# Mixture of experts in a decoder trunk: the pairs of experts in a software pipeline on TensorE

## The chip, the cores and the metric

The kernel runs on one core of a Trainium2 chip. The metric is device time in microseconds (us), the median over runs; lower is better. PE is TensorE, DVE is VectorE, ACT is ScalarE, POOL is GpSimd, and SP is the engine that issues nearly all transfers here.

## What is computed

Two layers of a hybrid decoder over 256 tokens of 1024 features, all in float32. The change lies in the mixture of experts at the end of each layer, which in the reference is:

```
weights = sel / jnp.sum(sel, axis=-1, keepdims=True)          # two experts of 16 for each token
combine = jnp.sum(jax.nn.one_hot(idx, N_EXPERTS) * weights[..., None], axis=1)
def add_expert(acc, p):
    e_w1, e_w3, e_w2, e_c = p                                  # 1024 x 512, 1024 x 512, 512 x 1024
    y = (jax.nn.silu(hf @ e_w1) * (hf @ e_w3)) @ e_w2
    return acc + e_c[:, None] * y, None
```

The rest of a layer (four mixers, gates, the router) is not touched.

## The kernel before

The 16 experts are worked in eight pairs (expert e with e + 8), each pair on 128 slots: four groups of 32 slots, each group on its own quarter of PE's columns. The work of a pair has these steps, and the texts below use these names:

- **gather** (`gather`, once for two pairs): eight blocks of the slots' tokens, feature-major, by a one-hot matrix (L1506 on PE, evacuated in turn by DVE L1510 and ACT L1508); the one-hot transposed (L1521, copied by ACT L1522); the slots' weights (DVE L1514 and L1515, added by POOL L1516, then L1526 on PE).
- **first products** (L1560): eight weight pages, two banks. Then `swiglu`: tanh on ACT (L1473) and two DVE operations (L1474, L1475).
- **transposes** of the hidden activations (`turn`: L1483 on PE into one bank, copied by ACT L1485).
- **second products** (L1584): four weight pages, two banks; DVE scales them (L1591), ACT and DVE split them in high and low halves (L581, L582).
- **token sums** (`combine`): for four pieces of the output, two matmuls (L1537) into one bank each, which DVE adds to x (L1538).

The weights come as 96 pages of 1 MB per layer. `order` lists them, `issue` sends them through SP's queue as soon as a page of SBUF is free, and `done` frees a page after its last matmul. Eight banks of PSUM are shared out by tags: `acc` has three, `mx` two, `rw` three. First products take two of `acc`, second products two of `mx`, the transposes one of `rw`, token sums one of `acc` at a time, a gather `mx` and `rw`. The order of instructions on an engine is not the order of the code: the framework's scheduler places them, and every engine then works its own list strictly in that order, each instruction waiting for its inputs and its bank.

Ahead of the last pair's transposes stands `tc.If(ov > 0)`, a branch of every engine over `dense`, a slow path for counts that the slots can't hold. It isn't entered here, so a branch is taken past it. After the last pair comes the next layer's norm, or the output.

Of the kernel before, what the change touches and what calls it, by code (L numbers as in the profile page):

```python
"""Hybrid decoder trunk: S5, sparse attention, RG-LRU and RWKV-7 mixers, gated merge, grouped MoE."""
# [13 lines left out]
F32R = mybir.dt.float32r                 # 12 significant bits: a float32 is exactly the sum of two  # L15
AF = mybir.ActivationFunctionType
OP = mybir.AluOpType
# [3 lines left out]
P = 128  # L21
L, D, T = 2, 1024, 256
W = 256
KT = D // P
NE, NPAIR, DE = 16, 8, 512
EARLY = [(0, 0), (1, 0)]                 # modulation values by PE instead of DVE: layer, group
NW = 2                                   # buffers of halves of weights
NR, NM = 5, 15                           # pages of 8 KB per partition: of the weight stream, of everything else
KEEP = 1                                 # pages of the latter that the stream leaves free
FILL, SPARE = (2, 2, 2, 2, 1, 3, 3), 2   # work beside the mixers: steps of it per step of them, pages it leaves free  # L30
XAT, MAT_AT = 3, 3                       # pages of the stream that x and the small matrices follow
PLAN = "1311330100b0322d22ac"            # that work: gates of a branch (0 to 3), its merge (a to d)
PSB = dict(acc=3, mx=2, rw=3)            # banks of PSUM: dense products, small ones, RWKV
TM = (164, 256, 256, 256)                # columns of iq | ik | iw, of q, k and v
# [5 lines left out]
# Columns of the per-feature parameters of a layer: name, number of columns.  # L40
# [9 lines left out]
# Small matrices of a layer, side by side.  # L50
# [27 lines left out]
class Pages:  # L78
    """Pages of [128, 2048] float32 in SBUF, whole or in slots of 512; the longest free goes first."""

    def __init__(self, pool, name, n):
        self.tiles = [pool.tile([P, 2048], F32, tag=f"{name}{i}", name=f"{name}{i}") for i in range(n)]
        self.free_pages = list(range(n))
        self.slots = []                 # free slots of split pages: (page, slot)
        self.used = {}                  # page -> slots in use, of split pages
        self.owner = {}
# [60 lines left out]
def _emit(ctx, tc, I, out):  # L147
# [26 lines left out]
    # ------------------------------------------------------------------ weight stream  # L174
# [3 lines left out]
    def fill_plan(l):  # L178
        """What runs beside the mixers: the gates, and modulation values that are needed later."""
# [16 lines left out]
    for l in range(L):  # L196
# [12 lines left out]
        for pr in range(NPAIR):  # L209
            for kt in range(KT):  # L210
                order.append((("w13", l, pr, kt), I["w13"][l, pr, kt], 2048))
            for ft in range(4):
                order.append((("w2", l, pr, ft), I["w2"][l, pr, ft], 2048))
# [37 lines left out]
    # ------------------------------------------------------------------ inputs and constants  # L251
# [45 lines left out]
    # Masks of 64 x 64 tiles: rows (p mod 64) are s, columns t; t > s, t >= s, and the blocks that  # L297
    # the recursive inverse joins.
# [17 lines left out]
    # Slots of a pair (e, e + 8) of experts: 32..95 and then 0..31 for e, 96..127 and then 0..31 for e + 8.  # L316
# [3 lines left out]
    # Of four, an earlier one (last index) also goes before an equal one.  # L320
# [8 lines left out]
    # ------------------------------------------------------------------ small accurate functions  # L329
# [22 lines left out]
    def sincos(sn, cs, ang, shape):  # L352
        """Reduction by quarter turns in parts that multiply exactly, then polynomials."""
# [1188 lines left out]
    def experts(l, x, oh, sid, wts, used, regi, gate2):  # L1542
        now, nxt, last = {}, {}, None
        steps = gather(l, 0, sid, used, nxt)
        for pr in range(NPAIR):
            i = pr % 2
            if i == 0:
                now, nxt = nxt, {}
# [242 lines left out]
```

## Time and profile before

| what | value |
|---|---|
| median of 3 runs | 1261.74 us (1261.24 to 1262.14) |
| span of the profiled execution, from its first to its last instruction | 1258.4 us |
| median of the runs above that span | 3.3 us |
| PE busy | 1105.5 us (88%) |
| DVE busy | 752.8 us (60%) |
| mean rate of transfers | 262 GB/s |

The experts are the stretches from about 399 to 646 us (layer 0) and from about 1002 to 1248 us (layer 1). Times inside the trace are counted from the span's start. An instruction of the program that takes float32 operands shows as two records on PE.

### The profile page before, as it was taken

What the parts mean: (1) busy time and instruction counts of PE and PEld (TensorE: products, weight loads), DVE (VectorE), ACT (ScalarE), POOL (GpSimd) and SP (SyncE); (2) the same over time, 40 slices, a digit from 0 to 9 for tenths busy, and PEclk for the clock granted to TensorE, in tenths of its full rate; (3) what the DMA queues carried; (4) which work ended last, traced back from release to release, by engine and by line L of the source; (5) the groups of instructions that cost most, each with busy time, mean ns of one, the idle gap of its engine ahead of it and who ended that gap; (6) DMA issues with size and microseconds to landing.
All of it is one profiled execution on the core that took longest, in us unless ns stands there. A gap on an engine that the chain in (4) does not pass through costs nothing. (4 is left out here: it accounts for less than half of the span.)

```text
span 1258.4 us, 22758 instructions
## 1 busy us (share of the span) xinstructions
PE 1105.5 (88%) x9286; PEld 722.1 (57%) x9286; DVE 752.8 (60%) x1439; ACT 374.1 (30%) x662; POOL 257.5 (20%) x320
## 2 busy tenths in 40 slices
PE   3878999988986999998849899998898699999894
PEld 0878886856873345332218798886677444443321
DVE  5789995598666134232275899959877623233223
ACT  1543433415432111110026544541354211011101
POOL 0593112151232000000091111115414200000000
PEclk8888999989997999998969899999899799999897
DMA  9635787625564999999803468832346489999951
GB/s 357 232 126 208 294 304 292 244 70 199 179 255 150 362 407 421 421 421 410 323 34 134 137 235 299 302 135 101 140 177 255 165 323 416 421 420 420 419 223 52
DMA packets 47089, 329.83 MB, mean 262 GB/s; under 512 B 5992, under 2 KB 6120, under 8 KB 7552
## 3 DMA queue, kind: packets, MB, share of 16 engines
q1 hardware_dynamic: 45776, 327.47, 66.9%
q8 instruction: 78, 1.28, 0.4%
q10 hardware_dynamic: 1200, 0.79, 0.2%
q14 instruction: 35, 0.29, 0.1%
HBM read 327.19 MB, written 1.05 MB: 261 GB/s over the span
## 5 line engine op out<-in xcount | busy, mean ns | idle before, releaser
L614 PE MATMUL acc<-h_hi,whi 128*128 128x256 f32 x720 | 213.8, 297 | 0.2 <-ACT whi L581 0.2
L614 PE MATMUL acc<-h_hi,wlo 128*128 128x256 f32 x720 | 206.3, 287 | 3.5 <-DVE wlo L582 3.5
L614 PE MATMUL acc<-h_lo,whi 128*128 128x256 f32 x720 | 206.4, 287 | 3.3 <-DVE h_lo L582 3.3
L582 DVE TENSOR_TENSOR wlo<-ring,whi 128x1024 fp32r<-128x1024 f32 (+2 forms) x122 | 152.6, 1254 | 62.7 <-ACT whi L581 54.7
L581 ACT ACTIVATE whi<-ring 128x1024 fp32r<-128x1024 f32 (+2 forms) x122 | 125.9, 1033 | 208.9 <-PE acc L614 145.9
L1560 PE MATMUL acc<-page,page 128*32 128x512 f32 (+1 forms) x1408 | 174.3, 600 | 0.0
L614 PEld LDWEIGHTS acc<-h_hi,whi 128*128 128x128 f32 x720 | 138.6, 192 | 16.8 <-issue 7.4
L614 PEld LDWEIGHTS acc<-h_lo,whi 128*128 128x128 f32 x720 | 139.0, 193 | 7.4 <-DVE h_lo L582 4.1
L614 PEld LDWEIGHTS acc<-h_hi,wlo 128*128 128x128 f32 x720 | 139.0, 193 | 6.7 <-DVE wlo L582 4.5
L1560 PEld LDWEIGHTS acc<-page,page 128*32 128x32 f32 x1408 | 48.8, 110 | 95.2 <-issue 90.8
L1591 DVE SCALAR_TENSOR_TENSOR page<-mx,moslw,page 128x512 f32<-128x512 f32 x32 | 24.0, 751 | 124.9 <-PE mx L1584 124.9
L1584 PE MATMUL mx<-page,page 128*32 (+1 forms) x704 | 87.4, 630 | 5.2 <-ACT page L1485 5.2
L1560 PE MATMUL acc<-ring,page 128*32 128x512 f32 (+1 forms) x640 | 84.7, 595 | 0.0
L468 DVE SCALAR_TENSOR_TENSOR page<-ring,csil,page 128x512 f32<-128x512 f32 x112 | 83.0, 780 | 0.0
L1516 POOL TENSOR_TENSOR page<-page,page 128x512 f32<-128x512 f32 x6 | 7.6, 1271 | 328.4 <-DVE page L1515 233.2
L1538 DVE TENSOR_TENSOR page<-page,acc 128x512 f32<-128x512 f32 x64 | 41.7, 683 | 51.9 <-PE acc L1537 51.2
L1474 DVE SCALAR_TENSOR_TENSOR page<-page,acc 128x512 f32<-128x512 f32 x16 | 11.0, 687 | 96.9 <-ACT page L1473 96.9
L1584 PEld LDWEIGHTS mx<-page,page 128*32 128x32 f32 x704 | 24.1, 116 | 59.3 <-issue 49.1
L581 ACT ACTIVATE wlo<-page 128x512 fp32r<-128x512 f32 x32 | 20.2, 631 | 123.5 <-DVE page L1591 123.5
L1473 ACT ACTIVATE page<-acc 128x512 f32<-128x512 f32 x16 | 9.6, 597 | 154.2 <-PE acc L1560 154.2
L1317 POOL TENSOR_TENSOR page<-page,page 128x512 f32<-128x512 f32 x21 | 32.3, 1557 | 79.3 <-DVE page L1315 78.3
L1537 PE MATMUL acc<-wlo,whi 128*128 128x512 f32 x128 | 44.7, 438 | 2.3 <-ACT wlo L581 1.4
(514 smaller groups left out, 2102.8 us busy)
## 6 DMA issues: line engine op xcount, KB each, us to landing
page<-in_w SPq DMA_DIRECT2D x132, 1024.0 KB, 12.1
ring<-in_w SPq DMA_DIRECT2D x60, 1024.0 KB, 11.3
ring<-in_ada_w SPq DMA_DIRECT2D x48, 1024.0 KB, 5.2
ring<-in_gate_w SPq DMA_DIRECT2D x32, 1024.0 KB, 5.8
ring<-in_branch_w SPq DMA_DIRECT2D x8, 1024.0 KB, 4.8
ring<-in_w_rw SPq DMA_DIRECT2D x6, 1024.0 KB, 10.2
ring<-in_w_tm SPq DMA_DIRECT2D x6, 1024.0 KB, 4.8
ring<-in_w_fm SPq DMA_DIRECT2D x6, 1024.0 KB, 4.8
```

The source lines that it names most:

```text
L468: V.scalar_tensor_tensor(p[:, js], w[:, js], csil[:, kt, 0:1], p[:, js], op0=OP.mult, op1=OP.add)
L581: S.activation(hi, a, AF.Copy)
L582: V.tensor_tensor(lo, a, hi.bitcast(F32), OP.subtract)
L614: PE.matmul(p, w, x_, **f)
L1317: G.tensor_tensor(mix[dp], mix[dp], t, OP.add)
L1473: S.activation(a, h1, AF.Tanh, scale=0.5)
L1474: V.scalar_tensor_tensor(b, a, 1.0, h1, op0=OP.add, op1=OP.mult)
L1537: PE.matmul(p, oh[:, P * a:P * a + P], y[:, fs], start=y is yh, stop=y is yl)
L1538: V.tensor_tensor(x[:, a, fs], x[:, a, fs], p, OP.add)
L1560: PE.matmul(hh[f][32 * g:32 * g + 32, :], xg[:, kt, P * i + 32 * g:P * i + 32 * g + 32], w[:, ds(offs[g] + 512 * f, 512)], start=kt == 0, ...
L1584: PE.matmul(yp[f][32 * g:32 * g + 32, :], gT[:, ft, 32 * g:32 * g + 32], w[:, ds(offs[g] + 512 * f, 512)], start=ft == 0, stop=ft == 3)
L1591: V.scalar_tensor_tensor(t, yp[f], now["w"][:, i:i + 1], gate2[:, fs], op0=OP.mult, op1=OP.mult)
```

## The change

The loop over pairs is cut in two functions, `first(pr)` (gather, first products, swiglu) and `second(pr)` (transposes, second products, halves), and put together so that the code runs first(0); then for each pair first(pr + 1), the token sums of pair pr - 1, second(pr); and the last token sums at the end. Every gather now goes block by block beside the first products of its own even pair; before, this was so for pair 0 alone, and the others were written as a block ahead of the transposes of an odd pair. First products of odd pairs go to `rw` instead of `acc`, transposes of odd pairs to `acc` instead of `rw`. The branch stands after the token sums of pair 6. The pages are listed in the new order of use. Nothing that is computed changes, and no instruction of the path that is taken is added or removed.

```
-        for pr in range(NPAIR):
-            for kt in range(KT):
-                order.append((("w13", l, pr, kt), I["w13"][l, pr, kt], 2048))
-            for ft in range(4):
-                order.append((("w2", l, pr, ft), I["w2"][l, pr, ft], 2048))
+        for pr in range(NPAIR + 1):
+            if pr < NPAIR:
+                order.extend((("w13", l, pr, kt), I["w13"][l, pr, kt], 2048) for kt in range(KT))
+            if pr:
+                order.extend((("w2", l, pr - 1, ft), I["w2"][l, pr - 1, ft], 2048) for ft in range(4))
...
-    def turn(b):
-        p = pt("rw", [P, 4, P])
+    def turn(b, tag="rw"):
+        p = pt(tag, [P, 4, P])
...
     def experts(l, x, oh, sid, wts, used, regi, gate2):
-        now, nxt, last = {}, {}, None
-        steps = gather(l, 0, sid, used, nxt)
-        for pr in range(NPAIR):
-            i = pr % 2
+        packs, regs, hidden, outs = {}, {}, {}, {}
+
+        def first(pr):
+            i, pp = pr % 2, pr // 2
+            steps = None
             if i == 0:
-                now, nxt = nxt, {}
+                o = packs[pp] = {}
+                steps = gather(l, pp, sid, used, o)
...
-            hh = [pt("acc", [P, 512]) for _ in range(2)]
+            hh = [pt("rw" if i else "acc", [P, 512]) for _ in range(2)]
             for kt in range(KT):
-                if pr == 0:
+                if steps:
                     next(steps)
...
-            b = swiglu(hh[0], hh[1])
-            if last:
-                combine(x, *last)
-            if i:
-                M.free(xg)
-                if pr + 1 < NPAIR:
-                    for _ in gather(l, (pr + 1) // 2, sid, used, nxt):
-                        pass
-            if pr == NPAIR - 1:
...
-            gT = turn(b)
+            hidden[pr] = swiglu(hh[0], hh[1])
+
+        def second(pr):
+            i, o, offs = pr % 2, packs[pr // 2], regs.pop(pr)
+            gT = turn(hidden.pop(pr), "acc" if i else "rw")
...
+            outs[pr] = o["oh"][:, i], yh, yl
+
+        first(0)
+        for pr in range(NPAIR):
+            if pr + 1 < NPAIR:
+                first(pr + 1)
+            if pr:
+                combine(x, *outs.pop(pr - 1))
+            if pr == NPAIR - 1:
...
+            second(pr)
```

Three places of PE's list show what the scheduler made of it. In the listing, x4 counts instructions of the program that read alike, one weight page is four rows of products with their ISA rows between, and the changed kernel's lines L1564, L1581 and L1602 are L1560, L1584 and L1576 of the kernel before.

Before, the end of the third gather (pairs 4 and 5) and pair 3's transposes (rw_4651), on PE in layer 0:

```order
L1526 MATMUL rw_4645<-ones_f,page_78 128x1 x4
L1483 MATMUL rw_4651<-identr,page_78 128x128 x2
L1506 MATMUL mx_4627<-whi_4578,h_hi 128x256
L1506 MATMUL mx_4627<-whi_4578,h_lo 128x256
L1506 MATMUL mx_4627<-whi_4578,h_hi 128x256
L1506 MATMUL mx_4627<-whi_4578,h_lo 128x256
L1483 MATMUL rw_4651<-identr,page_78 128x128 x2
L1584 ISA
L1584 MATMUL mx_4657<-page_85,page_78 32x512 x4
```

Now, the end of pair 4's first products and pair 3's transposes (acc_4730), on PE:

```order
L1564 MATMUL acc_4565<-ring_67,page_85 32x512 x4
L1564 ISA
L1564 MATMUL acc_4566<-ring_67,page_85 32x512 x4
L1537 MATMUL acc_4726<-wlo_4554,whi_4198 128x512
L1537 MATMUL acc_4726<-wlo_4555,whi_4198 128x512
L1483 MATMUL acc_4730<-identr,page_77 128x128 x4
L1581 ISA
L1581 MATMUL mx_4736<-ring_68,page_78 32x512 x4
```

The gather has left this place: its blocks stand between pair 4's first products. Pair 3's transposes follow the token sums of pair 2, and its second products follow them with nothing between.

Before, the slots' weights of the fourth gather (rw_5014) and pair 5's transposes (rw_5020), on PE:

```order
L1506 MATMUL mx_4996<-whi_4947,h_hi 128x256
L1506 MATMUL mx_4996<-whi_4947,h_lo 128x256
L1506 MATMUL mx_4996<-whi_4947,h_hi 128x256
L1506 MATMUL mx_4996<-whi_4947,h_lo 128x256
L1526 MATMUL rw_5014<-ones_f,page_78 128x1 x4
L1483 MATMUL rw_5020<-identr,page_78 128x128 x4
L1584 ISA
L1584 MATMUL mx_5026<-ring_67,page_78 32x512 x4
```

Now, the same weights (rw_5074), on PE:

```order
L1521 MATMUL rw_5067<-identr,whi_4936 128x128 x4
L1581 ISA
L1581 MATMUL mx_4885<-ring_70,page_76 32x512 x4
L1581 ISA
L1581 MATMUL mx_4886<-ring_70,page_76 32x512 x4
L1526 MATMUL rw_5074<-ones_f,page_78 128x1 x4
L1581 ISA
L1581 MATMUL mx_4885<-ring_66,page_76 32x512 x4
```

They now stand one weight page deep in pair 4's second products, and pair 5's transposes are elsewhere, ahead of the last page of pair 6's first products.

Before, PE ahead of the branch: the end of pair 7's first products:

```order
L1560 MATMUL acc_5221<-ring_69,page_76 32x512 x4
L1560 ISA
L1560 MATMUL acc_5222<-ring_69,page_76 32x512 x4
L1574 TENSOR_LOAD moregi_3886
L1576 COMPARE_AND_BRANCH
```

Now, PE ahead of the branch:

```order
L1581 MATMUL mx_5250<-page_82,page_76 32x512 x4
L1537 MATMUL acc_5293<-wlo_5285,whi_4936 128x512
L1537 MATMUL acc_5297<-wlo_5285,whi_4936 128x512
L1537 MATMUL acc_5301<-wlo_5285,whi_4936 128x512
L1537 MATMUL acc_5305<-wlo_5286,whi_4936 128x512
L1600 TENSOR_LOAD moregi_3886
L1602 COMPARE_AND_BRANCH
```

Pair 7's first products are done much earlier, and the branch follows the second products and the token sums of pair 6. Pair 7's transposes stand right behind the branch in both.

## Rows read from the trace of the kernel before

**Rows 1.** The page: span, granted clock and transfer rate in 40 slices.

```profile
span 1258.4 us, 22758 instructions
PEclk8888999989997999998969899999899799999897
GB/s 357 232 126 208 294 304 292 244 70 199 179 255 150 362 407 421 421 421 410 323 34 134 137 235 299 302 135 101 140 177 255 165 323 416 421 420 420 419 223 52
```

**Rows 2.** Windows: busy time of each engine (instructions), PE's granted clock, DMA share.

```profile
399.00:500.00 101.00, 100.52 (x827) 43.75 (x827) 30.20 (x58) 13.37 (x23) 2.54 (x2) 0.98 0.94 372
500.00:625.38 125.38, 116.84 (x903) 41.16 (x902) 35.87 (x62) 15.34 (x26) 2.54 (x2) 0.96 0.97 401
1002.00:1102.00 100.00, 99.47 (x821) 43.11 (x820) 30.00 (x65) 14.18 (x25) 2.54 (x2) 0.98 0.92 373
1102.00:1229.77 127.77, 119.22 (x918) 42.64 (x912) 37.86 (x65) 15.71 (x27) 2.55 (x2) 0.96 0.88 362
```

**Rows 3.** Waits of PE, 1002 to 1246 us: total us, times, longest.

```profile
PE rw L1483 <- issue: 3.9, 1, 3.9
PE mx L1584 <- ACT page L1485: 3.8, 5, 0.9
PE rw L1526 <- POOL page L1516: 3.0, 1, 3.0
PE rw L1483 <- DVE page L1475: 1.4, 1, 1.4
...
PE acc L1537 <- ACT wlo L581: 0.7, 1, 0.7
PE acc L1537 <- DVE wlo L582: 0.4, 1, 0.4
```

**Rows 4.** Timeline of PE, layer 1: start, us, line, [idle before, releaser].

```profile
1112.73 3.54 PE L1584 MATMUL mx<-ring,page 128*32 x16 [0.92 <-ACT page L1485]
...
1173.86 1.70 PE L1526 MATMUL rw<-ones_f,page 128*128 128x1 f32 x8 [2.99 <-POOL page L1516]
...
1177.27 5.42 PE L1584 MATMUL mx<-page,page 128*32 x32 [0.75 <-ACT page L1485]
1182.51 1.89 PE L1584 MATMUL mx<-ring,page 128*32 x16
...
1187.76 0.73 PE L1537 MATMUL acc<-wlo,whi 128*128 128x512 f32 x2
...
1197.72 5.33 PE L1560 MATMUL acc<-page,page 128*32 x48
1204.42 0.66 PE L1483 MATMUL rw<-identr,page 128*128 128x128 f32 x4 [1.37 <-DVE page L1475]
1205.77 3.64 PE L1584 MATMUL mx<-page,page 128*32 x32 [0.69 <-ACT page L1485]
```

**Rows 5.** Windows in which the granted clock was 0.50, layer 1.

```profile
1112.60:1116.00 3.40, 3.27 (x16) 0.79 (x20) 0.00 (x0) 0.08 (x1) 0.00 (x0) 0.50 1.02 424
1174.10:1180.90 6.80, 6.05 (x32) 3.01 (x35) 0.16 (x1) 0.60 (x1) 0.00 (x0) 0.50 1.01 418
1232.10:1238.90 6.80, 4.49 (x24) 1.46 (x27) 0.00 (x0) 0.60 (x1) 0.00 (x0) 0.50 0.20 70
```

**Rows 6.** Line L1576, the branch, on PE's queue: ns min/median/max, starts.

```profile
L1576 PEldq COMPARE_BRANCH x2: 3317/4109/4901, 623.1 to 1227.4; - x2
```

**Rows 7.** Timelines of DVE, POOL and ACT, layer 1.

```profile
1171.59 0.73 DVE L1515 TENSOR_SCALAR page<-slots,mosp,mowu 128x256 f32<-128x256 bf16 x2
1172.55 1.26 POOL L1516 TENSOR_TENSOR page<-page,page 128x512 f32<-128x512 f32 x1 [62.81 <-DVE page L1515]
...
1186.26 0.75 DVE L1591 SCALAR_TENSOR_TENSOR page<-mx,moslw,page 128x512 f32<-128x512 f32 x1 [0.17 <-PE mx L1584]
1202.26 0.60 ACT L1473 ACTIVATE page<-acc 128x512 f32<-128x512 f32 x1 [14.58 <-PE acc L1560]
1202.89 0.69 DVE L1474 SCALAR_TENSOR_TENSOR page<-page,acc 128x512 f32<-128x512 f32 x1 [6.12 <-ACT page L1473]
1203.68 0.69 DVE L1475 TENSOR_TENSOR page<-page,acc 128x512 f32<-128x512 f32 x1
```

More of the change, by code (lines that the diff above doesn't have):

```diff
@@ L1542, in experts @@
     def experts(l, x, oh, sid, wts, used, regi, gate2):
-        now, nxt, last = {}, {}, None
-        steps = gather(l, 0, sid, used, nxt)
-        for pr in range(NPAIR):
-            i = pr % 2
+        packs, regs, hidden, outs = {}, {}, {}, {}
+        def first(pr):
+            i, pp = pr % 2, pr // 2
+            steps = None
             if i == 0:
-                now, nxt = nxt, {}
+                o = packs[pp] = {}
+                steps = gather(l, pp, sid, used, o)
             rv = nc.values_load(regi[0:1, pr:pr + 1], engines=[ET.PE], min_val=0, max_val=1024,
                                 skip_runtime_bounds_check_because="it is 1024 times a comparison's result")
-            offs = (rv, 0, 0, 1024)
-            hh = [pt("acc", [P, 512]) for _ in range(2)]
+            offs = regs[pr] = (rv, 0, 0, 1024)
+            hh = [pt("rw" if i else "acc", [P, 512]) for _ in range(2)]
             for kt in range(KT):
-                if pr == 0:
+                if steps:
                     next(steps)
-                xg = now["xg"]
+                xg = packs[pp]["xg"]
                 w = get(("w13", l, pr, kt))
@@ L1562, in experts @@
                 done(("w13", l, pr, kt))
-            if pr == 0:
+            if steps:
                 next(steps, None)
-            b = swiglu(hh[0], hh[1])
-            if last:
-                combine(x, *last)
-            if i:
+            else:
                 M.free(xg)
-                if pr + 1 < NPAIR:
-                    for _ in gather(l, (pr + 1) // 2, sid, used, nxt):
-                        pass
-            if pr == NPAIR - 1:
-                ov = nc.values_load(regi[0:1, NPAIR:NPAIR + 1], min_val=0, max_val=1,
-                                    skip_runtime_bounds_check_because="it is a comparison's result")
-                with tc.If(ov > 0):
-                    dense(l, x, oh, wts, gate2)
-            gT = turn(b)
+            hidden[pr] = swiglu(hh[0], hh[1])
+        def second(pr):
+            i, o, offs = pr % 2, packs[pr // 2], regs.pop(pr)
+            gT = turn(hidden.pop(pr), "acc" if i else "rw")
             yp = [pt("mx", [P, 512]) for _ in range(2)]
@@ L1590, in experts @@
                 fs, t = slice(512 * f, 512 * f + 512), M.take([P, 512])
-                V.scalar_tensor_tensor(t, yp[f], now["w"][:, i:i + 1], gate2[:, fs], op0=OP.mult, op1=OP.mult)
+                V.scalar_tensor_tensor(t, yp[f], o["w"][:, i:i + 1], gate2[:, fs], op0=OP.mult, op1=OP.mult)
                 halves(yh[:, fs], yl[:, fs], t)
                 M.free(t)
-            last = now["oh"][:, i], yh, yl
+            outs[pr] = o["oh"][:, i], yh, yl
[6 more added lines that the diff above has]
+            if pr == NPAIR - 1:
+                ov = nc.values_load(regi[0:1, NPAIR:NPAIR + 1], min_val=0, max_val=1,
+                                    skip_runtime_bounds_check_because="it is a comparison's result")
+                with tc.If(ov > 0):
+                    dense(l, x, oh, wts, gate2)
+            second(pr)
         ss = square_sums()
-        combine(x, *last, ss)
+        combine(x, *outs.pop(NPAIR - 1), ss)
         return [rstd(ss, a) for a in range(2)]
```

## The prediction, made before the changed kernel was run

> **What bounds the kernel now.** I read the page first. Its rates [rows 1] show the two stretches of experts as the only places where transfers run at some 420 GB/s, so the first question is whether weights or PE set their pace. In the list of PE's waits over layer 1's experts, of which [rows 3] show the larger ones, no wait ends with a transfer. While the last pair works, the transfers have dropped to a share of 0.20, against 1.01 some 55 us earlier [rows 5]: the weights are all there before PE wants them. Had PE wanted them faster, it could have had them. So PE's list, with its waits, is the chain here.
>
> The windows cut at the end of pair 7's products (625.38 and 1229.77 us) show where PE loses time [rows 2]. In the first 100 us of each layer's experts it is idle for 0.5 us; in the second part for 125.38 - 116.84 = 8.5 us (layer 0) and 127.77 - 119.22 = 8.6 us (layer 1). So up to the branch there are 9.1 us per layer to be had, nearly all behind pair 2. They have few places [rows 3, 4]: 0.92, 0.69, 0.75 and 0.69 us where second products wait for ACT's copy of the transposes (four of the five waits of that row), 2.99 us where the fourth gather's weights wait for POOL, 1.37 us where pair 6's transposes wait for its swiglu, and crumbs.
>
> A second loss does not look like idleness. After the waits of 0.92 and of 2.99 us PE's granted clock is 0.50, the 1.2 GHz level, for 3.4 and 6.8 us [rows 5]. The reader sees it in the durations: 16 second products take 3.54 us at 1112.73 and 1.89 us at 1182.51 [rows 4]. PE was busy for 3.27 and 6.05 us of these windows, and half of that is lost: 1.6 + 3.0 = 4.7 us per layer. The third window, behind the branch, costs 4.49 / 2 = 2.2 us. Waits of 1.37 and 0.69 us between dense products, at 1204, brought no such fall.
>
> **What the change removes.** A swiglu, its transposes and their copy now have 64 first products of another pair, some 14 us, between them and their use in most pairs. The order shows which. Pair 6's transposes stand inside pair 7's first products and pair 5's ahead of pair 6's last page, so neither their swiglu (1.37) nor their copy (0.69 and 0.75) is waited for. The block of gather ahead of pair 3's transposes, behind which the clock fell, is dissolved among first products. The 2.99 us before the fourth gather's weights are a chain: swiglu's last DVE operation, two of L1515 (0.73), POOL's L1516 (1.26) [rows 7].
>
> **What stays or is added, up to the branch, per layer.**
> - Pair 0: between transposes and second products stand two small matmuls of a gather; of the 0.69 us copy some 0.3 stays.
> - Pair 3: second products directly behind the transposes, 0.7. Pairs 1 and 3 also take a bank of `acc` for their transposes. By the list of waits it is one that tanh and L1474 give back, at 1203.58 where products end at 1197.72 + 5.33 = 1203.05 [rows 4, 7], 0.5 us after the products; the token sums put ahead take 0.73 [rows 4]. So nothing is waited for. If the bank were one that waits for all of swiglu and a sum's addition, it would be 1.3 us each; that is the other end, 2.6 us.
> - Fourth gather: its L1521 directly follows pair 5's first products and waits for a bank until L1474, 0.6 by the same rows. Then L1521 and one page of second products run while DVE ends swiglu (1.3 us after the products), does L1515 twice (0.7) and POOL adds (1.5 with its start, 1172.32 to 1173.86): 3.6 us, against some 0.6 + 0.6 + 1.7 = 2.9 on PE. So 0.7 is left, 1.3 with the bank. If neither overlaps it is the 2.99 of before.
> - Behind pair 4's second products two blocks of gather want the two `mx` banks, and pair 6's first page wants the first block. DVE scales twice, splits once, then evacuates: 0.3 for the bank, 0.6 for the block.
> - Token sums of pair 5 begin directly behind its second products: 0.7, as for the last pair [rows 3].
> - Crumbs of 0.2 as before: 0.4.
>
> Sum 4.3 us, bounds 2.5 and 7.
>
> **The branch.** Before, 3.9 us in layer 1 and 2.9 in layer 0 passed between the last first products and the last transposes. This reads like the wait for swiglu that the change removes elsewhere, but swiglu accounts for no more than 1.4 us (as for pair 6). PE's own branch takes 3.3 and 4.9 us [rows 6]. It began at 623.1 and 1227.4, that is 2.3 us ahead of the products' end, so it had a head start. The Trainium skill (Runtime: NRT & Kernel Launch, Instruction fetch mechanics) says that a taken branch out of the fetched window must fetch its target before execution goes on; so read, the wait stays, while read as a wait for swiglu it would shrink and give 2 us more per layer. I keep it whole on the rows. In front of the branch now stand pair 6's second products and their token sums: the sums expose 0.7 + 0.4 us [rows 3] that pair 7's first products used to hide, and the branch, behind sums that wait, starts with less of its head start. That costs from 0 to 2.3 us. I take 0.8: most of the head start goes (1.7), but every us that PE waits inside the half-clock window behind the branch saves about half a us there. The branch thus adds 1.9 us per layer. Its fall of the clock stays.
>
> **Clock.** The waits that remain between dense products are shorter than 1.4 us, as the ones at 1204 that cost nothing. I count the 4.7 us as gained.
>
> **Transfers.** DVE, ACT and POOL do the same work in other places. SP sends the same pages in the new order of use. At 420 GB/s a page takes 2.5 us, a pair 30, and PE took (1229.77 - 1002) / 8 = 28.5 per pair; the stock built up ahead of the experts and the waits of before leave a margin. The rate falls in the slice that begins at 1195 [rows 1], at 223 / 420 of 31.5 us, so the last page came at about 1212, some 20 us ahead of its use. A layer that is 8 us faster still finds it there. Cost nothing; if the cover were gone, each page would cost up to 0.8 us, the 2.5 less the 1.7 to 1.8 of one page of products [rows 4].
>
> **Sum.** Per layer 9.1 - 4.3 - 1.9 + 4.7 = 7.6 us, for two layers 15.2. The span was 1258.4 [rows 1], and the median of the runs lies 3.3 above it: 1258.4 - 15.2 + 3.3 = 1246.5 us.
>
> **Rivals.**
> *The clock falls as often as before*, in other places. For it: a wait of 0.92 us sufficed once. Against it: that one followed a long block of gather, which is now spread. Gain 2 x (7.6 - 4.7) = 5.8, time 1256. The Trainium skill (TensorE: Matmul & The Clock Gate, A second HAM failure mode) says that small idle times while PE cycles through PSUM banks are enough to make the clock swing. By that rule this rival would win, since token sums still go through one bank beside first products of even pairs. In the stretch from 1185.94 to 1203 where sums do just that, the trace before shows no idle PE and no fall.
>
> *Slower: more falls than before.* The place is the short waits of the second half: pair 3's transposes, the fourth gather, the sums of pair 5. The longer of the two windows costs 3.0 us. With falls at all three the layer loses 9.0 instead of 4.7, so it is 2.9 + 4.7 - 9.0 = -1.4, and the time 1264.5. It decides when falls cost over 7.6 per layer, that is from the third one. Against it: of the waits at 0.7 us, only those behind a gather were near a fall.
>
> *The change doesn't do what it says.* The scheduler had already put the next pair's first products ahead of transposes in the early pairs, and the idle 0.5 us there shows that nothing is to be had. If the new waits take 7 us, the branch 3.4 with its whole head start, and one fall of 3 us stays, the layer gains 9.1 - 7 - 3.4 + 1.7 = 0.4: 1261, no change.
>
> *All hidden.* Only the sums ahead of the branch stay exposed: 9.1 + 4.7 - 1.1 = 12.7 per layer, 1236.
>
> **Chances.** Forecast 0.60, with its own range 1241 to 1254 from the bounds of the waits, the branch and one fall left. Clock as before 0.14, slower 0.08, no change 0.10, all hidden 0.08. The range 1238 to 1257 takes in the forecast, most of the second and part of the last. A measurement here tells changes over 0.2%, 2.5 us. Faster by more: 0.60 + 0.14 + 0.08 = 0.82; within 0.10; slower 0.08.
>
> **What would show it.** In the profile after, PE's waits for POOL and for L1475 should be gone or under 1 us, and idle time up to the branch near 4.3 us per layer. The clock should be 1.00 from the first products to the branch in both layers. The wait behind the branch should be there, at 3 to 6 us, with new waits of pair 6's sums before it. Wrong would be: half clock in the middle of the experts, a wait for a transfer, or a transposes' wait for a bank over 1 us.

## The result, and the profile after the change

The changed kernel takes 1244.24 us (median of 4 runs, 1243.88 to 1247.3), the kernel before 1261.49 in the same session: a ratio of 0.9874, 95% interval 0.9848 to 0.9900, so 1.0 to 1.5% faster. 1246.5 was predicted; the medians gained 17.25 us where 15.2 were forecast. The profiled execution took 1244.33 us. These lines of its page answer to [rows 1].

```profile
span 1242.6 us, 22769 instructions
...
PEclk8898999998997999999978899999899889999998
...
GB/s 358 230 136 184 279 307 308 246 104 203 170 239 138 388 420 421 420 420 420 334 56 95 144 238 306 289 170 119 85 205 253 169 271 423 420 421 420 420 319 67
```

The span of the profiled executions is 15.8 us shorter; the prediction's sum was 15.2. The sum came out, but not all of its terms did. To see them I cut each layer's experts from the first gather product to the last token sum. Windows of the kernel before (columns as in [rows 2]), then its two branches, and the row of its timeline behind the second one:

```profile
397.84:643.48 245.64, 231.84 (x1808) 90.39 (x1808) 73.45 (x134) 32.82 (x56) 20.03 (x60) 0.96 0.89 361
1002.62:1247.88 245.26, 230.52 (x1808) 90.02 (x1808) 72.51 (x133) 31.87 (x55) 5.08 (x4) 0.96 0.84 342
...
623.05:627.95 4.90, 2.33 (x24) 0.52 (x16) 1.37 (x2) 0.60 (x1) 0.00 (x0) 1.00 0.51 165
1227.44:1230.76 3.32, 2.33 (x24) 0.52 (x16) 1.04 (x2) 0.60 (x1) 0.00 (x0) 1.00 0.02 7
...
1233.68 1.01 PE L1483 MATMUL rw<-identr,page 128*128 128x128 f32 x4 [3.90 <-issue]
```

The same windows of the changed kernel, with two that end where the token sums of pair 6 do, its two branches, and its only two stretches at half clock inside the experts (apart from the one in which each layer's experts begin, which both kernels have):

```profile
396.89:635.78 238.89, 224.59 (x1808) 87.69 (x1808) 73.64 (x134) 32.77 (x56) 21.47 (x63) 0.97 0.91 371
997.37:1232.04 234.67, 224.05 (x1808) 87.56 (x1808) 72.08 (x133) 31.90 (x55) 5.09 (x4) 0.98 0.87 357
...
399.00:613.14 214.14, 208.99 (x1725) 81.20 (x1723) 64.74 (x116) 28.75 (x49) 5.42 (x6) 1.00 0.97 398
1000.00:1213.76 213.76, 208.62 (x1722) 80.80 (x1721) 64.18 (x115) 28.28 (x49) 4.58 (x4) 1.00 0.95 390
...
612.81:619.20 6.39, 0.33 (x2) 0.00 (x0) 1.53 (x3) 0.00 (x0) 0.00 (x0) 0.74 1.01 388
1213.43:1217.28 3.85, 0.33 (x2) 0.00 (x0) 1.56 (x3) 0.00 (x0) 0.00 (x0) 0.91 0.27 106
...
615.80:626.00 10.20, 5.90 (x28) 1.90 (x32) 0.48 (x1) 0.60 (x1) 6.27 (x33) 0.50 0.41 152
1216.60:1223.40 6.80, 5.22 (x24) 1.71 (x28) 0.00 (x0) 0.60 (x1) 0.00 (x0) 0.50 0.01 2
```

Layer 0 is 6.8 us shorter (245.64 to 238.89), layer 1 10.6 (245.26 to 234.67). In both, PE's busy time fell by more than the clock alone gives, 7.2 and 6.5 us. Its idle time fell by 4.1 us in layer 1 (14.74 to 10.62), and rose by 0.5 in layer 0 (13.80 to 14.30): there the branch takes 6.39 us, and the last token sums wait 1.35 us for DVE's halves where they waited 0.36. Up to the branch the clock is 1.00, where [rows 5] had two stretches at 0.50.

PE's waits over layer 1's experts (990 to 1240 us), against [rows 3]:

```profile
PE acc L1483 <- PEq L1602: 3.7, 1, 3.7
PE acc L1537 <- ACT wlo L581: 3.1, 4, 0.8
PE mx L1581 <- ACT page L1485: 1.7, 3, 0.7
PE acc L1537 <- DVE wlo L582: 0.7, 3, 0.3
PE rw L1521 <- DVE page L1474: 0.6, 1, 0.6
PE rw L1526 <- POOL page L1516: 0.4, 1, 0.4
PE acc L1564 <- DVE page L1510: 0.3, 1, 0.3
```

The wait for POOL has shrunk from 3.0 to 0.4 us, and the one for L1475 is gone. Of the five waits for the transposes' copy three are left. Token sums wait for the halves four times instead of once: they now stand directly behind second products. The timeline of PE at the end of layer 1 shows the sums and the branch:

```profile
1186.01 0.50 PE L1537 MATMUL acc<-wlo,whi 128*128 128x512 f32 x1 [0.75 <-ACT wlo L581]
1186.49 1.92 PE L1564 MATMUL rw<-ring,page 128*32 x16
1188.35 1.78 PE L1537 MATMUL acc<-wlo,whi 128*128 128x512 f32 x6
...
1196.24 7.05 PE L1564 MATMUL rw<-page,page 128*32 x64
1203.11 1.90 PE L1581 MATMUL mx<-page,page 128*32 x16
...
1210.89 0.50 PE L1537 MATMUL acc<-wlo,whi 128*128 128x512 f32 x1 [0.74 <-ACT wlo L581]
1211.63 2.13 PE L1537 MATMUL acc<-wlo,whi 128*128 128x512 f32 x7 [0.23 <-DVE wlo L582]
1217.45 1.09 PE L1483 MATMUL acc<-identr,page 128*128 128x128 f32 x4 [3.69 <-PEq L1602]
```

### The profile page after: what moved, and what is told of

Read it like the earlier page. It is cut to its first block, busy times and chain, and to the rows that moved or that the text cites. A ratio compares the mean times of both kernels' runs of the same rounds, so it can differ in the third digit from the quotient of the medians.

```text
span 1242.6 us, 22769 instructions
## 1 busy us (share of the span) xinstructions
PE 1096.4 (88%) x9286; PEld 720.3 (58%) x9286; DVE 754.5 (61%) x1439; ACT 374.1 (30%) x662; POOL 255.2 (21%) x320
## 5 line engine op out<-in xcount | busy, mean ns | idle before, releaser
L1564 PE MATMUL rw<-page,page 128*32 (+1 forms) x704 | 86.5, 593 | 0.0
L1564 PE MATMUL acc<-page,page 128*32 (+1 forms) x704 | 84.6, 605 | 0.6 <-DVE page L1510 0.6
L1581 PE MATMUL mx<-page,page 128*32 128x512 f32 (+1 forms) x672 | 80.0, 622 | 2.0 <-ACT page L1485 2.0
L1516 POOL TENSOR_TENSOR page<-page 128x512 f32<-128x512 f32 x8 | 10.2, 1273 | 299.0 <-DVE page L1515 176.4
L1510 DVE TENSOR_SCALAR page<-mx,scale,shift 128x256 f32<-128x256 f32 x32 | 17.4, 544 | 82.7 <-PE mx L1506 82.7
L1564 PEld LDWEIGHTS rw<-page,page 128*32 128x32 f32 x704 | 28.4, 110 | 46.1 <-issue 41.7
L1474 DVE SCALAR_TENSOR_TENSOR page<-page,rw 128x512 f32<-128x512 f32 x8 | 5.5, 688 | 80.0 <-ACT page L1473 80.0
L1581 PEld LDWEIGHTS mx<-page,page 128*32 128x32 f32 x672 | 21.8, 114 | 54.5 <-issue 45.7
L1508 ACT ACTIVATE page<-mx,shift,scale 128x256 f32<-128x256 f32 x32 | 18.0, 563 | 104.3 <-PE mx L1506 104.3
```

The lines of the kernel that those rows point to most:

```text
L1508: S.activation(xg[:, kt], p, AF.Identity, scale=sc[:, kt:kt + 1], bias=sh[:, kt:kt + 1])
L1510: V.tensor_scalar(xg[:, kt], p, sc[:, kt:kt + 1], sh[:, kt:kt + 1], op0=OP.mult, op1=OP.add)
L1516: G.tensor_tensor(cw, cw, t, OP.add)
L1564: PE.matmul(hh[f][32 * g:32 * g + 32, :], xg[:, kt, P * i + 32 * g:P * i + 32 * g + 32], w[:, ds(offs[g] + 512 * f, 512)], start=kt == 0, ...
L1581: PE.matmul(yp[f][32 * g:32 * g + 32, :], gT[:, ft, 32 * g:32 * g + 32], w[:, ds(offs[g] + 512 * f, 512)], start=ft == 0, stop=ft == 3)
```

## The experiments

Every kernel ran beside the kernel before on one chip, A to D, E to H and I to L in a session each (before: 1259.4, 1261.3 and 1261.0 us); across sessions the ratios compare. Executions of one kernel lay up to 9 us from their median, in part with stretches that the change doesn't touch (the first gather product came at 395 to 404 us). So the ratios have intervals of some 0.3% to either side, and the lengths of the experts in the profiles, one execution each, tell more than the medians. Where the code of a layer is that of the change (both layers of I, layer 0 of G, layer 1 of H) they agree with it within 0.8 us. A to L are the names below.

| kernel | experts, layer 0, us | layer 1, us | median, us | ratio to before, 95% |
|---|---|---|---|---|
| before | 245.64 | 245.26 | 1261.5 | |
| the change | 238.89 | 234.67 | 1244.2 | 0.9874 (0.9848 to 0.9900) |
| A, spread gather only | 239.87 | 237.37 | 1245.3 | 0.9866 (0.9828 to 0.9903) |
| B, pipeline, gather in blocks | 239.05 | 237.59 | 1251.0 | 0.9916 (0.9889 to 0.9943) |
| C, banks of before | 239.53 | 236.60 | 1242.9 | 0.9854 (0.9820 to 0.9887) |
| D, branch ahead of pair 6's second products | 234.34 | 233.02 | 1237.4 | 0.9810 (0.9777 to 0.9843) |
| E, no branch | 229.41 | 228.63 | 1232.4 | 0.9784 (0.9744 to 0.9825) |
| F, branch behind pair 7's second products | 232.71 | 229.57 | 1231.1 | 0.9765 (0.9734 to 0.9796) |
| G, more transfers in layer 1 | 238.15 | 237.22 | 1247.0 | 0.9910 (0.9878 to 0.9943) |
| H, transfers held in layer 0 | 234.84 | 234.55 | 1241.3 | 0.9859 (0.9823 to 0.9895) |
| I, the change again | 239.25 | 234.62 | 1245.3 | 0.9872 (0.9845 to 0.9900) |
| J, one block of gather | 235.55 | 233.89 | 1245.3 (one run) | |
| K, POOL held | 238.54 | 234.35 | 1242.1 | 0.9841 (0.9809 to 0.9873) |
| L, F with POOL held | 232.95 | 229.44 | 1228.7 | 0.9744 (0.9718 to 0.9769) |

### A and B: the two halves of the change apart

A takes the kernel before and spreads the gathers; B takes the changed kernel and makes blocks of them again.

```
A, against before:
             if i == 0:
-                now, nxt = nxt, {}
+                now = {}
+                steps = gather(l, pr // 2, sid, used, now)
...
-                if pr == 0:
+                if i == 0:
                     next(steps)
...
B, against the change:
                 steps = gather(l, pp, sid, used, o)
+                if pp:
+                    for _ in steps:
+                        pass
+                    steps = None
...
```

Expected of A: 

> The kernel before, with one part of the change: every gather goes block by block beside the first products of its own even pair; the pairs are not pipelined, banks and order of pages are as before. Theory A (the ledger of the prediction: the half-clock stretches in the middle belong to waits right behind a block of gather, and the 3 us wait for POOL to its end): both clock stretches in the middle go (4.7 us a layer) and most of the waits of 0.9 and 3.0 us, while the waits between a pair's own swiglu, transposes and second products stay or grow somewhat. Time 1247 to 1252. Theory B (the falls follow any wait of 0.7 us or more ahead of an odd pair's second products, whatever stands before it): the falls stay, only the wait for POOL goes, 2 x 3 us: 1255 to 1259. In the profile: granted clock in 500 to 615 us 1.00 by A, under 0.98 by B.

Expected of B: 

> The changed kernel, with the gathers of pairs 2, 4 and 6 as a block again, ahead of their even pair's first products. The pair pipeline stays. Theory A: the blocks bring back waits (banks of mx, the sum by POOL) and at least one fall of the clock in each layer, some 3 to 7 us per layer: 1250 to 1258. Theory B (the pipeline alone removed waits and falls): the blocks cost only the waits for their own evacuations, under 1 us each: 1244 to 1248, granted clock 1.00 from the first products to the branch.

A window of A up to the branch of layer 1, with the clock in the third column from the end:

```profile
1001.00:1217.88 216.88, 210.00 (x1721) 81.07 (x1713) 63.75 (x115) 28.22 (x48) 4.05 (x4) 1.00 0.94 383
```

and A's waits there (1050 to 1240 us):

```profile
PE rw L1483 <- DVE page L1475: 2.8, 2, 1.5
PE mx L1581 <- ACT page L1485: 2.7, 5, 0.7
PE rw L1483 <- PEq L1573: 2.4, 1, 2.4
```

The same window of B:

```profile
1000.00:1214.44 214.44, 209.25 (x1717) 81.54 (x1705) 62.03 (x112) 28.19 (x48) 3.83 (x3) 1.00 0.95 389
```

Theory B of A's expectation falls: A keeps two waits of 1.4 and 1.5 us for its own swiglu, and of five for the copy three of 0.7 (two are of 0.3), and its clock is 1.00. Its time, 1245.3, lies 1.7 us below the range of theory A. In the execution of B that was profiled theory A of B's expectation falls too: the gathers are blocks, the clock is 1.00, and the waits are those of the changed kernel. **In the profiled executions, either half of the change alone removes both falls of the clock.** For B that was the third fastest of 11 (1245.46 us, mean granted clock 0.942 over the whole run); the eight slower ones show 0.935 to 0.939, and where they lost it isn't on record. So falls in them are not ruled out: B's median, 1251.0, is in theory A's range. Why it lies some 5 us above the changed kernel's (by the ratios), when B's experts are only 3 longer in the profile, stays open.

The gains don't add: the experts of both layers together are shorter by 13.7 us in A and by 14.3 in B, and by 17.3 with both. In the medians A is as fast as the whole change (0.9866 and 0.9874, with intervals that overlap): there the pipeline adds nothing that can be measured. What it adds in the profile is PE's work. Taking off half of what lay at 0.50, that is 221.8 and 221.5 us before (layers 0 and 1), 221.8 and 221.5 in A, 222.0 and 221.7 in B, but 219.7 and 219.4 in the changed kernel. Part of B's shows in two rows of its timeline:

```profile
1043.20 1.05 PE L1568 MATMUL acc<-page,page 128*32 x2
...
1045.30 1.07 PE L1568 MATMUL acc<-page,page 128*32 128x512 f32 x8
```

Between blocks of gather stand single pieces of a weight page; two products take as long there as eight, since the eight run four at a time, one on each quarter of PE's columns (their records start 7 ns apart).

### C: the banks

```
-            hh = [pt("rw" if i else "acc", [P, 512]) for _ in range(2)]
+            hh = [pt("acc", [P, 512]) for _ in range(2)]
...
-            gT = turn(hidden.pop(pr), "acc" if i else "rw")
+            gT = turn(hidden.pop(pr), "rw")
```

> The changed kernel with the banks of before: first products of all pairs in acc, all transposes in rw. Theory A (the bank of the transposes decides nothing, as the prediction took it): 1243 to 1246.5, the same waits. Theory C (the swap is what makes the pipeline possible, since two pairs' first products and the token sums would want five of three acc banks): the first products of each pair wait for the swiglu of the pair before and the token sums for a bank, 1 to 2 us at each of 7 pairs: 1258 to 1272.

Theory A, as to the time (1242.9, just below its range); but the waits are not the same. They lie in other places (pair 6's transposes wait 1.4 us for swiglu again, token sums wait 1.5 us for ACT's halves instead of 3.1), and the time is that of the change within the intervals. The swap of banks is worth nothing that can be measured.

### D, E and F: the branch

D moves the branch up to `pr == NPAIR - 2`, ahead of the sums of pair 5; F moves it behind `second(7)`; E drops it.

```
F, against the change:
-            if pr == NPAIR - 1:
...
             second(pr)
+            if pr == NPAIR - 1:
+                ov = nc.values_load(regi[0:1, NPAIR:NPAIR + 1], min_val=0, max_val=1,
...
+                with tc.If(ov > 0):
+                    dense(l, x, oh, wts, gate2)
```

D: 

> The changed kernel with the branch moved up, directly behind pair 7's first products and ahead of the token sums of pair 5 and of pair 6's second products. Theory A (the branch costs PE a time of its own, 3.7 and 6.2 us now, less the head start that it gets from products that are still running when it is reached; waits of the sums in front of it take the head start away): with dense products in front of it the exposed part is 2.9 to 3.9 us a layer as before the change, and pair 6's token sums (1.0 us) are hidden by pair 7's second products: 1238 to 1242. Theory D (the wait has a fixed length wherever the branch stands, 3.7 and 6.2): only the 1.0 us of the sums go, twice: 1241.5 to 1243.5. Theory E (half a clock behind the branch now falls on two pairs' second products instead of one, so that the stretch at 0.50 becomes longer): 1244 to 1248.

E: 

> The changed kernel without the branch (it leaves out the slow dense path, which these inputs don't enter). Theory A (the wait behind pair 6's token sums is PE's own branch, 6.2 us in layer 0 and 3.7 in layer 1, and the half clock behind it its follow-up): both waits go, 9.9 us, and with them some or all of the half-clock stretches of 10.2 and 6.8 us, worth 2 to 3 us a layer at most; pair 7's transposes come without a wait: 1227 to 1235. Theory F (the transposes behind the branch wait for something else as well, a bank or the sums): only a part goes, 1239 to 1243.

F: 

> The changed kernel with the branch moved down, behind pair 7's second products, ahead of the last token sums. Theory A (the branch has a length of its own, 3.3 to 4.4 us when few transfers run and 6.0 to 6.4 when they fill their engines, and starts some 2.3 us ahead of the end of dense products in front of it): exposed are 1.3 to 2 us in layer 1 and 2 to 4 in layer 0, and the waits of the last sums for their halves (0.7 + 0.3) lie under it; pair 6's sums (1.0) are hidden; the half clock falls on the last sums and the norm: 1230 to 1237. Theory D (a fixed exposed time wherever it stands): 1240 to 1243.

D's two branches, as windows:

```profile
603.69:609.73 6.04, 2.33 (x24) 0.52 (x16) 1.37 (x2) 0.60 (x1) 0.00 (x0) 1.00 1.01 418
1197.94:1204.21 6.27, 2.33 (x24) 0.52 (x16) 1.37 (x2) 0.60 (x1) 0.00 (x0) 0.98 1.01 418
```

Both lie where the transfers are full, and both are long, in layer 1 too. PE still works for 2.33 us inside them: that is the head start, back again. The exposed part, up to PE's next product 0.3 us behind the branch, is 4.0 and 4.3 us (slightly more than theory A's 3.9), and the time is just below its range. The stretch at half clock behind the branch is shorter, 3.4 us in each layer instead of 10.2 and 6.8, so theory E falls. Without the branch (E) no stretch at half clock is left between the first products and the last sums, and the experts of both layers are 15.5 us shorter than with it; the time is in theory A's range. F's branches and its wait behind the one of layer 1:

```profile
625.76:629.39 3.63, 2.33 (x24) 0.52 (x16) 1.96 (x3) 1.05 (x2) 0.00 (x0) 1.00 0.34 124
1212.76:1216.11 3.35, 2.33 (x24) 0.52 (x16) 1.70 (x3) 0.80 (x2) 0.00 (x0) 1.00 0.02 5
```

```profile
PE acc L1537 <- DVEq L1603: 2.4, 1, 2.4
```

In F the branch follows dense products (head start 2.33) and meets few transfers, so that only 1.3 and 1.0 us of it are exposed. Behind it the last sums go on waiting for DVE, which lets them go behind its own branch, when all its halves are done: PE is idle for 2.4 us in all, where E's sums wait 0.7 and 0.2 for their halves. F's time, 1231.1, is in theory A's range and the same as E's within the intervals, though its experts are 4.2 us longer than E's; the rest comes from the norm (K, below).

### G and H: is it the transfers that make the branch long?

```
G, order, layer 1 only:
+        if l == L - 1:
+            order.extend((("br", l, "extra", kt), I["w13"][l, 0, kt], 2048) for kt in range(8))
...
H, ahead() stops at the next layer's pages until:
+                if (pr, ft) == (NPAIR - 1, 0):
+                    pg.free_pages.insert(0, pg.free_pages.pop())
+                    state["first"] = pg
+                    state["stop"] = len(order)
+                    ahead()
...
```

G: 

> The changed kernel with eight more pages (8 MB) sent behind the last weights of layer 1, which nobody reads, so that transfers run while PE is at the branch of layer 1; layer 0 is as it was. Theory A (transfers make the branch long): the branch of layer 1 takes 6.0 to 6.4 us instead of 3.85, the time is 2 to 4 us longer than the changed kernel's: 1246 to 1249. Theory G (the branch of layer 0 is long because of what its code is, or because it is the first): layer 1 stays at 3.7 to 4.4 us, 1243 to 1246.

H: 

> The changed kernel, with the next layer's pages held back in layer 0 until pair 7's first page of second products is done, so that no transfer runs while PE is at the branch of layer 0; the transfers then start some 20 us later. Theory A: the branch of layer 0 takes 3.3 to 4.4 us instead of 6.4, the half clock behind it is shorter, and the pages still come before the mixers of layer 1 want them: 1239 to 1242. Theory G (as above): the branch stays above 6 us, 1243 to 1246. If the held pages come late instead, PE or DVE waits for a transfer between 640 and 680 us, and the time is 1245 or more.

G's branches, layer 0 and 1:

```profile
611.03:617.78 6.75, 0.32 (x2) 0.00 (x0) 1.55 (x3) 0.00 (x0) 0.00 (x0) 0.71 1.01 390
1208.22:1214.21 5.99, 0.33 (x2) 0.00 (x0) 1.57 (x3) 0.00 (x0) 0.00 (x0) 0.75 1.00 417
```

H's:

```profile
615.53:619.02 3.49, 0.33 (x2) 0.00 (x0) 1.55 (x3) 0.00 (x0) 0.00 (x0) 0.94 0.03 7
1209.44:1213.34 3.90, 0.33 (x2) 0.00 (x0) 1.55 (x3) 0.00 (x0) 0.00 (x0) 0.89 0.02 4
```

Theory A twice. Transfers that nobody reads lengthen the branch of layer 1 from 3.85 to 5.99 us (share 0.27 to 1.00), and that layer is 2.6 us longer; with the transfers held, the branch of layer 0 takes 3.49 instead of 6.39 (share 1.01 to 0.03), and that layer is 4.0 us shorter. Both times are in theory A's ranges, but by the intervals alone neither could be told from the change.

The record of transfers shows where the time goes. Of the packets in it some are of kind `instruction`; one queue moves them in pieces of 16 KB. This is its line in the page of the changed kernel:

```profile
q8 instruction: 78, 1.28, 0.4%
```

E, without the two branches, has 74, the others 77 or 78. In each of the 26 branches of the profiles such a packet ends shortly before the branch does. All times are in us:

| share of the transfers during the branch | branches | length | packet starts behind the branch's start | packet takes | branch ends behind it |
|---|---|---|---|---|---|
| at most 0.43 | 13 | 3.3 to 4.4 | 1.0 to 1.8 | 0.9 to 2.0 | 1.3 to 1.4 |
| 0.46 to 0.79 | 4 | 4.9 to 6.3 | 1.1 to 3.9 | 0.9 to 2.0 | 1.3 to 1.8 |
| 0.99 and more | 9 | 5.9 to 6.8 | 3.5 to 4.4 | 0.9 to 1.3 | 1.3 to 1.4 |

What full transfers lengthen is the time until the packet starts: from 1.31 us in layer 1 of the change to 3.64 in G, and from 4.04 in layer 0 to 1.08 in H. (Where there are several such packets, it is the last.) That this packet holds the code behind the branch is read from these times; the record doesn't say what is in it.

### I and J: the change again, and one block of gather

I is the changed kernel. J restores the old order at one place: the third gather as a block, pair 3's transposes and second products, and then `first(4)`.

```
...
-            if pr + 1 < NPAIR:
+            if pr + 1 < NPAIR and pr != 3:
                 first(pr + 1)
...
+            if pr == 3:
+                for _ in gather(l, 2, sid, used, packs.setdefault(2, {})):
+                    pass
...
             second(pr)
+            if pr == 3:
+                first(4)
```

I: 

> The changed kernel itself, as it is, beside the next three on one chip: 1241 to 1247, ratio to before 0.985 to 0.990.

J: 

> The changed kernel with the old order at one place: the third gather as a block behind the token sums of pair 2, then pair 3's transposes and second products, and only then pair 4's first products. Theory A (the clock falls where a wait of about 0.9 us directly follows a block of gather; neither a block nor such a wait does it alone): the granted clock falls to 0.50 once in the middle of each layer, at pair 3's second products, and costs 1.5 to 3 us a layer. Theory H (it takes several such waits in a row, or the wait for POOL of 3 us): clock 1.00 up to the branch in both layers.

I repeats the result. J decides nothing: there was no fall, but neither was there the wait behind the block that the test was to bring back, so a block and a wait together were not tried apart from the kernel before. What J adds to B is one more block with the clock at 1.00. It has one run alone; in its profile the experts of both layers are 4.1 us shorter than the changed kernel's, so the old order at this place costs nothing that shows.

### K and L: the norm behind the last sums

The middle part between the two layers' experts had become longer, 359.1 to 361.6 us. About the whole of it is PE's wait for the norm (12.3 us before, 14.9 now; 12.9 to 18.6 in the other profiles but F, K and L). K lets POOL begin its tables of layer 1 only when the norm is done; L does the same to F.

```
+        if l:
+            G.tensor_scalar(cs[:, :, 0:1], bc(rs[1][:, :, None], [P, 8, 1]), 0.0, 1.0, op0=OP.mult, op1=OP.add)
+        else:
             G.memset(cs[:, :, 0:1], 1.0)
```

K: 

> The changed kernel, with POOL's tables of layer 1 begun only when the norm at the end of layer 0's experts is done (their first operation reads its result). Theory P (the wait of PE for that norm, 12.3 us before the change and 14.9 after it, is long because DVE's small operations with two inputs wait for POOL's operations that run beside them): the wait falls to 5 to 7 us and the middle part between the experts from 361.6 to 353 to 356 us, 1235 to 1239; if POOL's tables then come late, up to 4 us of it go again. Theory Q (the norm's chain is long by itself): the wait stays over 11 us, 1243 to 1248.

L: 

> The kernel with the branch behind pair 7's second products, with POOL's tables held in the same way. There the wait for the norm was 7.8 us, POOL's tables having begun at small sizes at 629.6. Theory P: some 2 us less than 1231, 1227 to 1231. Theory Q: no change, 1229 to 1233.

DVE and POOL in the changed kernel, on the timeline (start, length):

```profile
642.57 0.16 DVE L338 SCALAR_TENSOR_TENSOR rs1t<-rs1t,ss 128x1 f32<-128x1 f32 x1
642.65 1.89 POOL L713 TENSOR_TENSOR page<-page,s5e 128x1024 f32<-128x1024 f32 x1
642.65 1.91 DVE L337 TENSOR_TENSOR rs1t<-rs1y 128x1 f32<-128x1 f32 x1
...
645.93 1.89 POOL L716 TENSOR_TENSOR page<-page,s5e 128x1024 f32<-128x1024 f32 x1
646.00 1.83 DVE L337 TENSOR_TENSOR rs1t<-rs1y 128x1 f32<-128x1 f32 x1
```

and DVE's in K:

```profile
643.85 0.16 DVE L337 TENSOR_TENSOR rs1t<-rs1y 128x1 f32<-128x1 f32 x1
...
644.12 0.15 DVE L337 TENSOR_TENSOR rs1t<-rs1y 128x1 f32<-128x1 f32 x1
```

An operation of DVE on one column ends when POOL's ends, at 1.91 instead of 0.15 us. With POOL held PE's wait falls to 6.4 us: theory P. The middle part is 356.7 us, just above its range. But the time, 1242.1, is in theory P's range only with the 4 us that it allowed for late tables, and it cannot be told from the change beside it (0.9841 and 0.9872, with intervals that overlap). K's waits of PE from 634 to 700 us show one place of it, the weights' halves for the next products (2.0 us in the changed kernel, 4.9 here):

```profile
PE mx L574 <- ACT page L567: 6.4, 1, 6.4
PE acc L616 <- DVE wlo L582: 4.9, 3, 2.8
```

In F this wait was 7.8 us, since the branch that releases POOL stands 9.8 us ahead of the norm's operations instead of 20.8, and POOL's pieces are still small there. L takes it to 6.1, but the wait for the halves grows from 2.8 to 6.5: between F and L no difference can be told (the intervals overlap, and the middle part is 354.3 us in both). L has the lowest median of all, 1228.7 us, which lies just below theory Q's range and in theory P's; by the overlap with F it decides nothing. D, E, F and L are all faster than the change.

## Why the prediction was right, and where its terms were not

What the terms of the sum became (us per layer, a gain positive):

| term | forecast | layer 0 | layer 1 |
|---|---|---|---|
| waits up to the branch, with the sums ahead of it | 3.7 | 3.9 | 3.9 |
| the wait behind the branch | -0.8 | -3.3 | 0.2 |
| the last second products and sums | 0 | -1.0 | 0.0 |
| half clock in the middle | 4.7 | 4.7 | 4.7 |
| the rest of PE's work | 0 | 2.5 | 1.8 |
| sum | 7.6 | 6.8 | 10.6 |

**The waits up to the branch** were predicted at 4.3 us per layer, and at 1.1 for the sums of pair 6: 5.4. The windows that end with these sums show 214.14 - 208.99 = 5.15 and 213.76 - 208.62 = 5.14. The single terms came too, with small differences: 0.27 for pair 0 (0.3), 0.69 for pair 3 (0.7), 0.58 and 0.37 at the fourth gather (1.3 with the bank), 0.31 for the block and bank behind pair 4 (0.9), 0.75 for the sums of pair 5 (0.7). One of 0.84, at the sums of pair 3, which stand one weight page behind pair 3's second products, was not foreseen; it makes up for the two that came out smaller.

**The clock** came back as counted, two stretches of 3.4 and 6.8 us in each layer, 4.7 us. The rival in which it falls elsewhere didn't come. The waits that are left, A's of 1.4 and 1.5 us between products and B's of 0.3 inside blocks of gather left the clock at 1.00. The Trainium skill (TensorE: Matmul & The Clock Gate, A second HAM failure mode) tells of a kernel in which PE is idle for short times so often, between groups of products that cycle through PSUM banks, that the clock swings. The waits here are few and far between, so no run here shows that case. My own reason, that the dissolved block does it, was half a reason: B's profiled execution shows a block without a wait behind it, A's such waits without a block, and neither falls. The kernel before has both together, and a second fall behind a wait of 2.99 us; that it takes both is argued from this, and no run forced it.

**The branch** is the term that was mis-sized, and luck hid it. "The branch thus adds 1.9 us per layer": the sums in front of it cost 0.97 of 1.1, but the wait behind them, which was to grow by 0.8, grew by 3.3 in layer 0 (2.9 to 6.2, more than the 3 to 6 that were to show it) and shrank by 0.2 in layer 1 (3.9 to 3.7). Three steps failed.

The first took the branch's length from [rows 6] as its own. It depends on the transfers that run meanwhile, and the change moved the branch of layer 0 from 623 us, where their share was 0.51, to 613, where it is 1.01: 4.90 us became 6.39. G and H moved the share alone, and the length followed. The Trainium skill (Runtime: NRT & Kernel Launch, Instruction fetch mechanics) says that a taken branch whose target isn't in the part fetched ahead waits until that is fetched; the packet of instructions in every branch agrees with this. That it starts late because it queues behind the weights is my reading; the rows show only that it starts late when weights move.

The second is the saving: 1.7 us of head start were to go, and about half of that was to come back from the half clock behind the branch. 2.0 us went (2.33 us of products inside the branch before, 0.33 now), and nothing came back: the work done at half clock there is 5.90 and 5.22 us, against 5.69 and 4.49 before.

The third read the whole wait of 3.9 us in layer 1 as the branch. Its own rows say otherwise: 3.32 us with a head start of 2.33 leave 1.0, and the branch was over at 1230.76, while the transposes ran only at 1233.68. Their first weights were loaded at 1231.21, and then PE stood for 2.33 us with nothing that the profile shows it to wait for. A 16 KB packet of instructions ran from 1231.50 to 1232.46 in this time; PE went on 1.2 us after it, much as it goes on behind a branch. A second fetch is thus likely, but no run tested it. (In layer 0 of F, 1.7 us among the last sums, also with nothing waited for, end 1.3 us after such a packet.) Of the other 25 branches none has such a wait directly behind it: PE goes on within 0.4 us, or waits for DVE (F, L). So in layer 1 the change lost 2.0 us of head start and 0.5 of length, and was spared 2.8 behind the branch; that these cancel is luck.

**Terms that were not in the sum.** PE's work fell by 7.2 and 6.5 us, 4.7 of it the clock's in the middle. Reckoned at the full clock, as at A and B, it fell by 2.1 to 2.2 us in each layer. In the timeline above 16 records of products (one weight page) between sums take 1188.35 - 1186.49 = 1.86 us, and 64 in a row 6.87, 1.72 for each 16: work done in fewer pieces would be less. This is argued from the rows; no run isolates it. Against it, the norm between the layers cost 2.6 us more. K shows that this wait is POOL's doing; that POOL's tables had come to larger pieces by then is read from the timeline, and 2.6 is less than the wait varies between the profiles. In layer 0 the last sums wait 1.0 us longer for DVE's halves, beside POOL's tables; no run isolates that.

**The step from span to median** was put at 3.3 us; a run's time lies 1.7 to 1.8 above its span in all runs here. The profiled execution of before, at 1258.4, was simply one of the faster. So of the 2.3 us by which 1246.5 was too high, 1.7 are this step and 0.6 the sum: 6.75 + 10.59 of the experts and 0.95 ahead of them, less 2.47 between them, is 15.8, against 15.2 predicted. The waits in front of the branch and the clock came as worked out; in the rest errors cancelled, and that the sum is so near is luck.

## What to carry to other kernels

Before moving work past a branch, look at two things in the profile: whether dense products stand right in front of it (here they hide 2.3 us), and what share the transfers have at that moment. Moved behind the last dense products, where the stream had run dry, the same branch cost 4.2 us of the two layers' experts, against 15.5 in the changed kernel. Compare the branch's own start and end with the wait behind it: what is left over is something else. Two edits that remove the same waits don't add up, so try each alone: here the spread gather, a few lines, gave all of the gain that the medians can show. And when a stage becomes shorter, compare the stage after it as well, because what other engines run beside it has shifted.

## What the hardware showed that I had not expected

- PE's taken branch takes 3.3 to 4.4 us with few transfers and 5.9 to 6.8 beside full ones. A 16 KB packet of instructions runs inside each; it starts 1.0 to 1.8 us after the branch with few transfers and 3.5 to 4.4 with full ones, and the branch ends 1.3 to 1.4 us after the packet (1.8 in one). Those of SP, ACT, POOL and DVE are recorded with 0.04 to 0.07 us.
- A DVE operation on 128x1 values with two inputs takes 0.15 us alone, and 1.91 when a POOL operation of 1.89 us starts in the same moment. The Trainium skill (SBUF — State Buffer, SBUF: two separate sides) has the two engines share a pair of ports under an exclusive lock, which a DVE operation with two inputs needs when POOL reads SBUF too. The rows agree: the two end within 0.02 us of each other.
